# A gated-attention trunk: keys and four gates of the second layer by seven block products for eight, their results kept in device memory, the rotary swap on ScalarE

## The chip, the core and the metric

The kernel runs on one core of a Trainium2 chip. The metric is device time in microseconds (us): the median of several runs of the whole program. The profile comes from one further execution of the same program. The engines are called PE (TensorE, matmuls; PEld is its weight load), DVE (VectorE), ACT (ScalarE), POOL (GpSimd) and SP (SyncE, which issues all DMAs here).

## The reference

The input is a sequence of 1024 positions with 1024 features, in float32. Layer one is gated linear attention; layer two is dilated sliding-window attention over keys and values that are shared by its heads. Cut to what matters here, layer two computes:

```python
kv = x @ w_kv                              # 6 key tiles of 128 features, 6 value tiles
k, v = split(kv)
k = rope(k, pos)                           # x1*cos - x2*sin, x2*cos + x1*sin over halves of 64
q, g = split(x @ w_in)                     # 8 heads x 3 groups of queries, 8 gate tiles
q = rope(q, pos) * HEAD_DIM ** -0.5
for window, dilation in ((128, 1), (512, 4), (2048, 16)):
    o_g, lse_g = dilated_window_attention(q[group], k[group], v[group], window, dilation)
o = sum(softmax(lse) * o_g)                # three groups joined
y = (o * silu(g)) @ w_out
x = layer_norm(alpha * x + y)
```

Two key heads serve eight query heads: heads 0 to 3 use key head 0, heads 4 to 7 use key head 1.

## The kernel before, in words

**Arithmetic.** A product of float32 matrices is made of three matmuls in the type fp32r: each operand is split into a high part (`split_hi`, L612, an ACT copy) and a low part (`split_lo`, L615, a subtraction on DVE or POOL), and high x high, high x low and low x high are summed in PSUM (`mm3`, L642). The attention itself uses plain float32 matmuls.

**Tiles.** Features lie on the 128 partitions and positions along the free dimension, in halves of 512. `project` (L655) makes one 128-feature tile of a projection: it loads 512 KB of weights, splits them (`load_w_now`, L629), and for each half runs 8 x 3 matmuls of 128x512 into one PSUM bank; a function `evac` then takes the bank out. `project_tok` (L664) and `proj_v` (L1218) make values with positions on the partitions. SBUF is handed out in pages of 128x1024 (`page`, L618, 16 of them in the pool `p0` and 16 in `p1`) and in halves of that (`small`, L1053).

**Order.** The program is not issued in the order in which it is written. The class `Sched` (L141) records every operation; `order` (L254) then lays them out by a list schedule with a cost for each operation (`cost`, L543), a rule that a POOL operation and a DVE operation with two SBUF operands don't run at once (`shares_port`, L532), a limit on buffers, and priorities: the program's order, moved forward by `WEIGHTS` for weight loads and by `EVAC` for taking banks out. Operations recorded on `S.vp` go to DVE or POOL, those on `S.va` to DVE or ACT. All instructions are issued from line 452, so the profile shows that line for nearly all of them, and groups must be told apart by tile names. Buffers of one tag are handed out in the program's order.

**Stages.** Layer one (`layer_a`, L725) takes four heads in turn. `gate` (L883) makes the running sum of the log decays by a scan with a mask that restarts it every 128 positions. Then `out_ln` (L1067) makes the output projection and the layer norm, for one half of the positions at a time, and `emit_a` (L1547) writes the result x1 to SBUF, split, and to device memory (`x1d`). Layer two (`layer_b`, L1176) follows:

1. values of the first half of positions (`proj_v(0)`, `proj_v0`), L1265;
2. six key tiles by `project`, each taken out by `rope` (L1194), L1267; `rows` (L1257) between them turns x1 for the last stage;
3. values of the second half, L1271; values of key head 0 come back from device memory in the order of their groups (`load_v`, L1243); keys and values of key head 1 go out to device memory (`kvd`) until head 3 is done (`reload_kv`, L1281);
4. eight heads, L1515: `scores(u)`, for u < 4 the gate projection `g_proj(u)`, the next head's three query projections `q_proj(u+1)`, `attend(u)` and, for u < 4, `close(u)`, which multiplies by the gate; the gates of heads 4 to 7 come afterwards.

`rope` takes a PSUM bank out by three DVE products, one with the cosines (128x512) and two with the sines (64x512 each, reading the other half of the partitions), and one sum on DVE or POOL that also writes the result in the order of its group (`to_group`, L1165), so that the attention reads it contiguously.

Last come the output projection and layer norm of layer two.

Of the kernel before, what the change touches and what calls it, by code (L numbers as in the profile page):

```python
# [17 lines left out]
NK = 8  # L18
# [17 lines left out]
AHEAD = 0.35  # L36
RUNS, GATHER = 0.3, 1.0


# [558 lines left out]
def trunk(tc, xT, wP, wA, wA12, wAv3, w2, wO, wK, wV0, wV12, wB, wOB, par_d,  # L598
# [4 lines left out]
    wts = S.pool("wts")  # L603
    p0 = S.pool("p0")
    ps = S.pool("ps", space="PSUM")
    dram = S.pool("dram", space="DRAM")
# [118 lines left out]
    def layer_a(t2, t1, after):  # L725
        lmask = t2.tile([128, NLEV - 2, 32], U8, name="lmask")
        smask = t2.tile([128, 512], F32, name="smask")

# [424 lines left out]
    x1t = [dram.tile([128, D], F32, name=f"x1t{k}") for k in range(4)]  # L1153
    kvd = [dram.tile([128, T], F32, name=f"kvd{i}") for i in range(4)]

# [20 lines left out]
    def layer_b(xs, early):  # L1176
# [11 lines left out]
        S.vector.tensor_copy(below, tri[:, 1:2])  # L1188
        cosT = page(p0, F32, "cosT")
        S.sync.dma_start(cosT, cos_d)  # L1190
        sinT = page(p0, F32, "sinT")
        S.sync.dma_start(sinT, sin_d)
# [10 lines left out]
        K = [[page(p0, F32, f"K{c}{g}") for g in range(3)] for c in range(2)]  # L1203
        V = [[None] * 3 for _ in range(2)]

        def proj_v0(blocks):
            for c in range(2):
                if V[c][0] is None:
                    V[c][0] = page(p0, F32, f"V{c}0")

            def evac(j, acc):
                S.scalar.activation(blk(V[0][0], j), acc[:, 0:128], AF.Copy)
                S.vector.tensor_copy(blk(V[1][0], j), acc[:, 128:256])
            project_tok(wV0, xs, [(j, lambda x, j=j: blk(x, j)) for j in blocks], evac)

        def proj_v(half):  # L1218
# [12 lines left out]
            with S.later(-EVAC):  # L1231
                pgs = [page(p0, F32, "Vn") for _ in range(2)]
# [30 lines left out]


        proj_v(0)  # L1265
# [5 lines left out]
        proj_v(1)  # L1271
        for g in (1, 2):
            load_v(0, g)
        rows(6)
        rows(7)
        proj_v0(range(4, 8))
        for g in range(3):
            S.sync.dma_start(kvd[g], K[1][g])
        S.sync.dma_start(kvd[3], V[1][0])

        def reload_kv():  # L1281
            for g in range(3):
                K[1][g] = page(p0, F32, f"K1{g}")
                S.sync.dma_start(K[1][g], kvd[g])
            V[1][0] = page(p0, F32, "V10")
            S.sync.dma_start(V[1][0], kvd[3])
            load_v(1, 1)
            load_v(1, 2)


        BL = {0: [(n * 128, max(n - 1, 0) * 128, 128 if n == 0 else 256) for n in range(8)],
# [11 lines left out]
        def q_proj(u):  # L1303
            Q = [page(p0, F32, "Q") for _ in range(3)]
            U[u]["Q"] = Q
            for g in range(3):
                project(wB[u, g], xs, lambda half, acc: rope(Q[g], g, half, acc))


        def g_proj(u):  # L1310
            sg = page(p0, F32, "sg")
            U[u]["sg"] = sg

            def evac(half, acc):
                th = small("th", "t1", 2)
                S.scalar.activation(th, acc, AF.Tanh, scale=0.5)
                S.vector.scalar_tensor_tensor(sg[:, hs(half)], th, 1.0, acc, op0=OP.add, op1=OP.mult)
            project(wB[u, 3], xs, evac)

# [7 lines left out]
        def scores(u):  # L1327
            Q, Kc = U[u]["Q"], K[u // 4]
            P = {}
            sts = hp.tile([128, 2, 24], F32, name="sts", bufs=2)  # L1330
            for g in (2, 1, 0):
                step = 8 if g == 2 else 2
                for j0 in range(0, 8, step):
# [11 lines left out]
                    for j in range(j0, j0 + step):  # L1345
# [6 lines left out]
                        if g < 2:  # L1352
                            S.tensor.matmul(sc[:, o:o + nk], Q[g][:, qc:qc + 128], Kc[g][:, kc:kc + nk],
                                             start=True, stop=True)
# [60 lines left out]
        def attend(u):  # L1415
            P, cw, Vc = U[u]["P"], U[u]["cw"], V[u // 4]
            og = page(p0, F32, "og")
            U[u]["og"] = og
# [109 lines left out]
        for u in (4, 5, 6, 7):  # L1528
            if u == 7:
# [14 lines left out]
    layer_a(t2, t1, reload_og)  # L1544
    x1s = []

    def emit_a(et, r, t):  # L1547
# [6 lines left out]
        split_lo(lo[:, r], t, hi[:, r])  # L1554
        S.sync.dma_start(x1d[et][:, r], t)

    for half in range(2):
# [43 lines left out]
def _arrays(inputs):  # L1601
# [46 lines left out]
    a["cos"] = c(np.concatenate([cs, cs]))  # L1648
    a["sin"] = c(np.concatenate([sn, -sn]))
    q, k = np.meshgrid(r(128), r(256), indexing="ij")  # L1650
# [35 lines left out]
```

## Time and profile before

| what | value |
|---|---|
| median of 3 runs | 1154.25 us (1153.87 to 1154.63) |
| span of the profiled execution | 1152.7 us |
| mean granted PE clock | 0.998 of full speed |
| DMA traffic | 108.39 MB, mean 94 GB/s |

How to read the profile: the busy table gives each engine's busy time, its share of the span and its instructions. The chain follows the work that ended last back to what released each step. The groups give, for instructions of one kind, operation and tile, their count, busy time and mean in ns, then the idle time of the engine before them and what ended it. A matmul's duration is its latency; the next one starts before it ends.

### The profile page before, as it was taken

To read this page: it belongs to the slowest core of one execution; us is meant where nothing else is said; L and a number is where in the kernel's file an instruction comes from. 1 tells how busy PE (TensorE), PEld (TensorE's weight loads), DVE (VectorE), ACT (ScalarE), POOL (GpSimd) and SP (SyncE) were. 2 spreads that over 40 slices of the span, in tenths; PEclk is the share of its full clock that TensorE was granted. 3 is DMA by queue.
4 is the path that set the end of the run, shared out by engine and by line. 5 is a ranking of instruction groups with operands and counts; after the bars stand their busy time and mean duration, and the time that the engine had idled before them with its cause. 6 is when DMAs were issued, how large, how long until landed. Compare 5 with 4: busy or idle time off the path is not lost.

```text
span 1152.7 us, 19731 instructions
## 1 busy us (share of the span) xinstructions
PE 1142.8 (99%) x7780; PEld 975.2 (85%) x7780; DVE 820.3 (71%) x1634; ACT 449.1 (39%) x929; POOL 188.0 (16%) x139
## 2 busy tenths in 40 slices
PE   9999999999999999999999999999999999999997
PEld 9888888889988888888988888888888888888876
DVE  6286862786966699764366868686777878767678
ACT  5355431646463335311214242424222443444342
POOL 1000100112011120211020303030211312212200
PEclk9999999999999999999999999999999999999999
DMA  7211222111144365443611111121141111134544
GB/s 256 71 38 38 74 79 87 38 61 51 57 171 140 137 214 158 166 143 103 208 47 34 51 38 57 38 50 45 38 165 39 38 21 38 39 96 126 193 136 182
DMA packets 93372, 108.39 MB, mean 94 GB/s; under 512 B 43648, under 2 KB 61952, under 8 KB 93280
## 3 DMA queue, kind: packets, MB, share of 16 engines
q1 hardware_dynamic: 93280, 107.13, 29.6%
q8 instruction: 61, 1.00, 0.4%
q14 instruction: 31, 0.25, 0.1%
HBM read 85.94 MB, written 21.17 MB: 93 GB/s over the span
## 4 chain that ended last, share of the span: by engine, by line
PE 93%; DVE 4%; DMA 2%; ACT 1%; issue 1%; POOL 0%; DVEq 0%; ACTq 0%
PE acc L452 63%; PE po L452 9%; PE lv L452 8%; PE vac L452 7%; PE ms L452 4%; PE pro L452 2%; DMA wf<-in_wOB 2%; DVE rt L452 1%; DVE wl L452 1%; DVE x1l L452 0%; ACT wh L452 0%; DVE P L452 0%; DVE lnA L452 0%; ACT woh L452 0%; DVE wol L452 0%
## 5 line engine op out<-in xcount | busy, mean ns | idle before, releaser
L452 PE MATMUL acc<-x1h,wh 128*128 128x512 f32 x608 | 252.3, 415 | 0.0
L452 PE MATMUL acc<-x1h,wl 128*128 128x512 f32 x608 | 237.6, 391 | 0.0
L452 PE MATMUL acc<-x1l,wh 128*128 128x512 f32 x608 | 237.1, 390 | 0.0
L452 ACT ACTIVATE wh<-wf 128x1024 fp32r<-128x1024 f32 (+2 forms) x104 | 108.1, 1040 | 281.0 <-PE acc L452 194.8
L452 POOL TENSOR_TENSOR wl<-wf,wh 128x1024 fp32r<-128x1024 f32 x39 | 93.5, 2397 | 553.1 <-ACT wh L452 414.8
L452 ACT ACTIVATE P<-P,sts 128x128 f32<-128x128 f32 (+2 forms) x192 | 81.5, 426 | 139.6 <-DVE sts L452 139.3
L452 PEld LDWEIGHTS acc<-x1h,wl 128*128 128x128 f32 x608 | 114.1, 188 | 24.5
L452 PEld LDWEIGHTS acc<-x1l,wh 128*128 128x128 f32 x608 | 114.5, 188 | 21.3
L452 PEld LDWEIGHTS acc<-x1h,wh 128*128 128x128 f32 x608 | 114.4, 188 | 21.1
L452 DVE TENSOR_TENSOR wl<-wf,wh 128x1024 fp32r<-128x1024 f32 (+2 forms) x66 | 83.4, 1265 | 58.2 <-ACT wh L452 48.0
L452 PE MATMUL acc<-xh,wh 128*128 128x512 f32 x256 | 101.8, 397 | 0.0
L452 PE MATMUL acc<-xh,wl 128*128 128x512 f32 x256 | 99.8, 390 | 0.0
L452 PE MATMUL acc<-xl,wh 128*128 128x512 f32 x256 | 99.7, 390 | 0.0
L452 DVE TENSOR_TENSOR t<-acc,cosT 128x512 f32<-128x512 f32 x60 | 41.4, 689 | 65.7 <-PE acc L452 65.7
L452 DVE TENSOR_TENSOR t<-acc,sinT 64x512 f32<-64x512 f32 x120 | 82.5, 688 | 1.6
L452 PE MATMUL lv<-K,Q 128*64 128x64 f32 (+2 forms) x512 | 70.2, 286 | 0.0
L452 DVE CUSTOM_DVE_ANT_0 P<-lv,bmask 128x256 f32<-128x256 f32 (+1 forms) x128 | 46.7, 379 | 25.1 <-PE lv L452 23.7
L452 PEld LDWEIGHTS lv<-K,Q 128*128 128x128 f32 (+1 forms) x512 | 53.8, 163 | 10.0 <-issue 1.6
L452 PE MATMUL acc<-ogh,wh 128*128 128x512 f32 x152 | 60.1, 395 | 0.0
L452 PE MATMUL acc<-ogh,wl 128*128 128x512 f32 x152 | 59.2, 389 | 0.0
L452 PE MATMUL acc<-ogl,wh 128*128 128x512 f32 x152 | 59.2, 389 | 0.0
L452 PEld LDWEIGHTS acc<-xh,wl 128*128 128x128 f32 x256 | 48.0, 188 | 10.2
(252 smaller groups left out, 2233.4 us busy)
## 6 DMA issues: line engine op xcount, KB each, us to landing
wf<-in_wB SPq DMA_DIRECT2D x32, 512.0 KB
wf<-in_wA SPq DMA_DIRECT2D x24, 512.0 KB
wf<-in_wO SPq DMA_DIRECT2D x16, 512.0 KB
wf<-in_wOB SPq DMA_DIRECT2D x16, 512.0 KB
wf<-in_wV SPq DMA_DIRECT2D x12, 512.0 KB
res<-in_xT SPq DMA_DIRECT2D x16, 256.0 KB
x1d<-rt SPq DMA_DIRECT2D x16, 256.0 KB
out<-rt SPq DMA_DIRECT2D x16, 256.0 KB
```

Source lines behind the costliest of these rows:

```text
L452: getattr(handle[o.eng], meth)(*[conv(a) for a in args], **{k: conv(v) for k, v in kw.items()})
```

## The change

It has five parts.

1. **Seven products for eight.** The six key tiles and the gate tiles of heads 0 to 3 are made in five pairs by a scheme of Strassen's kind. A pair's weights are seen as blocks of (upper or lower four tiles of the model dimension) x (first or second feature tile), x1 as blocks of (upper or lower four tiles) x (first or second half of positions). `seven` makes seven block products of 4 x 3 matmuls each, on sums of blocks, instead of eight; four block results come out of sums of products.
2. **Sums of x1.** `sums` forms the four sums T1 to T4 of x1's blocks from the rows of the layer norm and from x1d read back, and keeps them split, in 16 pages of `p0`.
3. **Device memory.** All keys, the first group's values and the four gates go to device memory (`kd`, `vd0`, `sgd`) and come back before the heads that use them (`reload_kv(0)`, `reload_kv(1)`, `load_gate`). All four value projections come first, then the sums, then pairs of keys and gates in turn, with `rows` between.
4. **Rotary swap.** In `rope` the two sine products become two ACT copies that swap the halves of the partitions and one product on DVE or POOL. Group 1's queries are no longer reordered when written; the scores load them with a step of four elements.
5. **Room.** The cosine and sine pages, the pages `og` and the staging of keys lie in a new pool of four pages; the cosines load from 200 us on; the scan's mask is half as long, so each scan becomes two; a scratch area is made smaller.

The diff, cut to its core:

```diff
+    def spare(dt, name):
+        return px.tile([128, T], dt, name=name, tag="pg", bufs=4)
...
-                S.vector.tensor_tensor_scan(b[:, r], smask, mn, 0.0, op0=OP.mult, op1=OP.add)
+                for c0 in (0, 256):
+                    S.vector.tensor_tensor_scan(b[:, half * 512 + c0:half * 512 + c0 + 256], smask,
+                                                 mn[:, c0:c0 + 256], 0.0, op0=OP.mult, op1=OP.add)
...
-        def rope(pg, g, half, acc):
+        def rope(pg, g, half, acc, walked=(0, 1, 2)):
             r = hs(half)
             t1 = small("t1", "t1", 2)
             S.vector.tensor_mul(t1, acc, cosT[:, r])
             t2 = small("t2", "t2", 2)
-            S.vector.tensor_mul(t2[0:64, :], acc[64:128, :], sinT[64:128, r])
-            S.vector.tensor_mul(t2[64:128, :], acc[0:64, :], sinT[0:64, r])
-            S.vp.tensor_add(to_group(pg, g, half), tok_view(t1, g), tok_view(t2, g))
+            S.scalar.copy(t2[0:64, :], acc[64:128, :])
+            S.scalar.copy(t2[64:128, :], acc[0:64, :])
+            S.vp.tensor_mul(t2, t2, sinT[:, r])
+            if g in walked:
+                S.vp.tensor_add(to_group(pg, g, half), tok_view(t1, g), tok_view(t2, g))
+            else:
+                S.vp.tensor_add(pg[:, r], t1, t2)
...
+        def load_pair(src):
+            with S.later(-WEIGHTS):
+                a, b = (wts.tile([128, 1024], F32, name="wf", bufs=2) for _ in range(2))
...
+                a11, a12 = split(a)
+                hi, lo = (small("w22", "a", 13, FR) for _ in range(2))
+                split_hi(hi, b[:, R])
+                split_lo(lo, b[:, R], hi)
+                a22 = four(hi), four(lo)
+                S.vp.tensor_add(b[:, R], b[:, L], b[:, R])
+                S.vp.tensor_sub(b[:, L], a[:, L], b[:, L])
+                s3, s1 = split(b)
+                S.vp.tensor_sub(a[:, L], b[:, R], a[:, L])
+                S.vp.tensor_sub(a[:, R], a[:, R], a[:, L])
+                s2, s4 = split(a)
+            return dict(P1=a11, P2=a12, P4=a22, P7=s3, P5=s1, P6=s2, P3=s4)
...
+        def seven(src, evac):
+            w = load_pair(src)
...
+            acc = prod("P1", "a")
+            u = small("u1", "a", 13)
+            with late():
+                S.scalar.copy(u, acc)
+            acc = prod("P7", "b")
+            f = small("u2", "a", 13)
+            with late():
+                S.scalar.copy(f, acc)
+            acc = prod("P2", "a")
+            with late():
+                evac(0, 0, acc)
+            prod("P4", "b")
+            acc = prod("P5", "c")
+            with late():
+                S.vector.tensor_add(f, f, acc)
+            acc = prod("P6", "d")
+            with late():
+                S.vector.tensor_add(u, u, acc)
+                c21 = small("c", "a", 13)
+                S.vector.tensor_add(c21, u, banks["b"])
+                evac(1, 0, c21)
+                S.vp.tensor_add(f, u, f)
+                evac(1, 1, f)
+            acc = prod("P3", "c")
+            with late():
+                S.vector.tensor_add(u, u, acc)
+                evac(0, 1, u)
...
         proj_v(0)
         proj_v0(range(4))
+        proj_v(1)
+        proj_v0(range(4, 8))
+        sums()
...
         for g in range(3):
-            for c in range(2):
-                project(wK[2 * g + c], xs, lambda hf, acc, p=K[c][g]: rope(p, g, hf, acc))
-                rows(2 * g + c)
...
+            keys(g)
+            for et in range(3 * g, min(3 * g + 3, 8)):
+                rows(et)
+            if 2 * g < NG:
+                gates(2 * g)
...
+        reload_kv(0)
...
-            if u < 4:
-                g_proj(u)
...
-                if u < 4:
+                if u < NG:
+                    load_gate(u)
                     close(u)
             if u == 3:
-                reload_kv()
-        for u in (4, 5, 6, 7):
+                reload_kv(1)
+        for u in range(NG, 8):
...
+    def sums():
+        for k in range(4):
+            t, low = raws[k], raws[k + 4]
+            old, old2 = (small("old", "d", 4) for _ in range(2))
+            S.sync.dma_start(old, x1d[k][:, 0:512])
+            S.sync.dma_start(old2, x1d[k + 4][:, 0:512])
+            S.vp.tensor_sub(old, t, old)
+            keep("T1", k, old)
+            S.vp.tensor_sub(t, low, t)
+            keep("T3", k, t)
+            S.vp.tensor_sub(low, low, old)
+            keep("T2", k, low)
+            S.vp.tensor_sub(old2, old2, low)
+            keep("T4", k, old2)
```

`keep` splits a sum into its page. NG is 4; a further switch for queries by the same scheme, NQ, is 0, so the queries stay as they were.

More of the change, by code (lines that the diff above doesn't have):

```diff
@@ L37 @@
 RUNS, GATHER = 0.3, 1.0
+NG, NQ = 4, 0
 class Buf:
@@ L1188, in layer_b @@
         S.vector.tensor_copy(below, tri[:, 1:2])
[L1189 to L1192, printed above, removed]
-        def rope(pg, g, half, acc):
+        cosT, sinT = spare(F32, "cosT"), spare(F32, "sinT")
+        with S.hold(200.0):
+            S.sync.dma_start(cosT, cos_d)
+            S.sync.dma_start(sinT, sin_d)
+        def rope(pg, g, half, acc, walked=(0, 1, 2)):
             r = hs(half)
@@ new lines, in pure, with prod, late @@
+        def pure(k0, h):
+            return [(xs[k0 + k][0][:, hs(h)], xs[k0 + k][1][:, hs(h)]) for k in range(4)]
+        MOVING = dict(P1=lambda: pure(0, 0), P2=lambda: pure(4, 0), P3=lambda: pure(4, 1),
+                      **{p: lambda n=n: [quarter(n, k) for k in range(4)]
+                         for p, n in (("P4", "T4"), ("P5", "T1"), ("P6", "T2"), ("P7", "T3"))})
+        def seven(src, evac):
+            w = load_pair(src)
+            banks = {}
+            def prod(p, bank):
+                first = bank not in banks
+                if first:
+                    tag = {"a": "acc", "b": "lv", "c": "po", "d": "acc"}[bank]
+                    banks[bank] = ps.tile([128, 512], F32, name="sev", tag=tag, bufs=2)
+                acc = banks[bank]
+                hi, lo = w[p]
+                for k, (xh, xl) in enumerate(MOVING[p]()):
+                    with S.group():
+                        S.tensor.matmul(acc, hi[:, k, :], xh, start=first and k == 0, stop=False, skip_group_check=True)
+                        S.tensor.matmul(acc, hi[:, k, :], xl, start=False, stop=False, skip_group_check=True)
+                        S.tensor.matmul(acc, lo[:, k, :], xh, start=False, stop=(k == 3), skip_group_check=True)
+                return acc
+            def late():
+                return S.later(-EVAC)
+            acc = prod("P1", "a")
[25 more added lines that the diff above has]
+                evac(0, 1, u)
@@ L1262, in rows, with sigmoid_gate, keys @@
                 S.sync.dma_start(x1t[i][:, et * 128:et * 128 + 128], blk(t, i))
+        def sigmoid_gate(sg, acc):
+            th = small("th", "t1", 2)
+            S.scalar.activation(th, acc, AF.Tanh, scale=0.5)
+            S.vector.scalar_tensor_tensor(sg, th, 1.0, acc, op0=OP.add, op1=OP.mult)
+        def keys(g):
+            for c in range(2):
+                K[c][g] = spare(F32, f"K{c}{g}")
+            seven([wK[2 * g], wK[2 * g + 1]], lambda c, hf, acc: rope(K[c][g], g, hf, acc))
+            for c in range(2):
+                S.sync.dma_start(kd[c][g], K[c][g])
@@ L1312, in g_proj, with load_gate @@
             U[u]["sg"] = sg
[L1314 to L1318, printed above, removed]
+            project(wB[u, 3], xs, lambda half, acc: sigmoid_gate(sg[:, hs(half)], acc))
+        def load_gate(u):
+            sg = page(p0, F32, "sg")
+            U[u]["sg"] = sg
+            S.sync.dma_start(sg, sgd[u])
         def pieces(P, g, j0):
```

97 lines of the change are left out of this document (66 added, 31 removed).

## The prediction

> **What bounds the kernel now.** I read the page's busy table and chain first, then the chain in order of time, then the busy time by stage, then the groups by form.
>
> ```profile
> PE 1142.8 (99%) x7780; PEld 975.2 (85%) x7780; DVE 820.3 (71%) x1634; ACT 449.1 (39%) x929; POOL 188.0 (16%) x139
> ...
> PE 93%; DVE 4%; DMA 2%; ACT 1%; issue 1%; POOL 0%; DVEq 0%; ACTq 0%
> ...
> q1 hardware_dynamic: 93280, 107.13, 29.6%
> ```
>
> TensorE (PE) is busy for 99% of the span and carries 93% of the chain that ended last; the DMA engines are three tenths full. A busy PE may still be half empty, since matmuls overlap, so the chain in order of time (start, length, what, count) has to say at what pace they are issued:
>
> ```profile
> 453.32 22.42 PE acc L452 x144
> 476.18 10.91 PE acc L452 x48
> ...
> 498.88 10.91 PE acc L452 x48
> ...
> 532.93 21.80 PE vac L452 x96
> ...
> 718.57 1.08 PE lv L452 x32
> ...
> 720.52 2.23 PE po L452 x20
> ...
> 779.49 1.08 PE lv L452 x32
> ...
> 889.09 1.50 PE lv L452 x34
> ...
> 939.20 1.50 PE lv L452 x34
> ```
>
> One projection of one 128-feature tile is 2 halves x 8 tiles of the model dimension x 3 partial products = 48 matmuls, and takes 10.91 us: one matmul of 512 columns every 0.227 us. It is a steady stream with nothing between, in the stage that the change rewrites. So a matmul taken away there is worth its pace, provided that the other engines keep up. How near they are shows in the busy time by stage (window, length, then busy time and count of PE, PEld, DVE, ACT, POOL):
>
> ```profile
> 429.00:453.00 24.00, 23.56 (x103) 18.87 (x102) 22.26 (x33) 12.60 (x21) 0.44 (x1) 1.00 0.47 158
> 453.00:464.00 11.00, 11.00 (x93) 10.96 (x93) 10.36 (x21) 7.63 (x14) 0.00 (x0) 1.00 0.88 274
> 464.00:498.00 34.00, 34.00 (x158) 28.30 (x158) 23.51 (x31) 7.81 (x12) 8.38 (x4) 1.00 0.48 154
> 498.00:532.00 34.00, 34.00 (x157) 28.16 (x157) 22.18 (x24) 4.63 (x6) 7.20 (x3) 1.00 0.34 108
> ...
> 889.00:939.00 50.00, 50.00 (x299) 43.09 (x298) 41.14 (x117) 18.31 (x63) 13.14 (x10) 1.00 0.14 33
> ```
>
> VectorE (DVE) is full up to 464 (the tail of the first layer norm), two thirds full in the key stage, four fifths in the attention heads. The granted clock is 1.00 throughout. DVE is the only engine that could take PE's place.
>
> **The matmuls removed.** Six key tiles and four gate tiles are 10 projections, 480 matmuls, 109.1 us by the row of 10.91. Afterwards they are five pairs; a pair is 7 products x 4 tiles x 3 partial products = 84 matmuls for 96. 420 x 0.2273 = 95.5 us. Gain: 60 x 0.2273 = **13.6 us**. The mean of one in the groups is no price for this:
>
> ```profile
> L452 PE MATMUL acc<-x1h,wh 128*128 128x512 f32 x608 | 252.3, 415 | 0.0
> L452 DVE TENSOR_TENSOR wl<-wf,wh 128x1024 fp32r<-128x1024 f32 x61 | 80.4, 1319 | 58.2 <-ACT wh L452 48.0 <-PE ms L452 9.7
> L452 POOL TENSOR_TENSOR wl<-wf,wh 128x1024 fp32r<-128x1024 f32 x39 | 93.5, 2397 | 553.1 <-ACT wh L452 414.8 <-PE ms L452 117.6 <-PE lv L452 12.1
> L452 DVE TENSOR_TENSOR t<-acc,cosT 128x512 f32<-128x512 f32 x60 | 41.4, 689 | 65.7 <-PE acc L452 65.7
> L452 DVE TENSOR_TENSOR t<-acc,sinT 64x512 f32<-64x512 f32 x120 | 82.5, 688 | 1.6
> L452 DVE TENSOR_TENSOR rt<-rt,R 128x512 f32<-128x512 f32 x24 | 16.0, 683 | 0.3 <-ACT R L452 0.3
> L452 DVE SCALAR_TENSOR_TENSOR sg<-th,acc 128x512 f32<-128x512 f32 x16 | 10.9, 683 | 5.1 <-ACT th L452 5.1
> L452 ACT ACTIVATE wh<-wf 128x1024 fp32r<-128x1024 f32 x100 | 105.7, 1058 | 280.9 <-PE acc L452 194.8 <-issue 44.1 <-PE vac L452 30.1
> L452 ACT ACTIVATE th<-acc 128x512 f32<-128x512 f32 x16 | 9.4, 588 | 20.6 <-PE acc L452 20.6
> ```
>
> and, from the view of the tile that the keys are written through (shortest, median, longest),
>
> ```profile
> L452 DVE TENSOR_TENSOR K<-t,t x12: 693/1412/2182, 473.3 to 534.7; 128x512 f32<-128x512 f32 x12
> ```
>
> 415 ns is one matmul's latency, of which the next hides almost half; 60 of those would be 24.9 us, which the pace above excludes.
>
> **What the pairs add on DVE.** These rows give the prices: 0.69 us for a sum or product of 512 columns, from PSUM or SBUF alike; 1.32 for a low part of 1024; and for the rotary sum, walked into the order of group 0, 1 and 2, I take the last row's three: 0.69, 1.41, 2.18. A pair splits three weight tiles and a half one (3 x 1.32 + 0.69 = 4.6), forms four block sums (2.7) and five sums of products (3.4). Keys add four cosine and four sine products (5.5) and four walked sums: 2.8, 5.6 or 8.7. That is 19.0, 21.8 and 24.9 us for the three key pairs. A gate pair adds four gating operations of 0.683 instead: 13.4. Together 92.5 us of DVE beside 95.5 us of PE: DVE just fits, if it did everything itself. It is really less, because operations overlap, and more where GpSimd (POOL) works, as the timeline shows:
>
> ```profile
> 429.49 0.39 PE L452 MATMUL vac<-wh,x1h 128*128 128x512 f32 x1
> ...
> 461.85 0.68 DVE L452 TENSOR_TENSOR rt<-rt,R 128x512 f32<-128x512 f32 x1
> 462.45 0.68 DVE L452 TENSOR_TENSOR x1l<-rt,x1h 128x512 fp32r<-128x512 f32 x1
> ...
> 470.54 0.55 DVE L452 TENSOR_SCALAR rt<-rt,par 128x512 f32<-128x512 f32 x1
> ...
> 476.69 2.40 POOL L452 TENSOR_TENSOR wl<-wf,wh 128x1024 fp32r<-128x1024 f32 x1 [3.58 <-ACT wh L452]
> ...
> 477.91 1.73 DVE L452 TENSOR_TENSOR K<-t,t 128x512 f32<-128x512 f32 x1
> ```
>
> Two DVE operations that last 0.68 start 0.60 apart, an eighth less than I counted, so about 82 us. And a walked sum that began while POOL held 2.40 us of work took 1.73 instead of 0.69. I take the first as the rule and the second for a rival. ScalarE's share, 3 x 1.06 + 0.63 of splits, two copies out of PSUM at 0.59 and, for keys, eight swap copies, is 9.7 us in a pair of 19.1: hidden. The copies that PE waits for inside a pair (a bank is copied between two products that accumulate in it) have one product, 12 x 0.227 = 2.7 us, as cover, against 0.59 and at most one split of 1.06 ahead in ScalarE's queue: nothing.
>
> **The sums of feature halves.** All four value projections now come first: 2 x 21.80 and 2 x 11.51 (the row of 22.42 less 10.91) = 66.6 us, from 429.5 to 496. Beside them DVE finishes the layer norm (to about 471, when the last row is scaled), splits six weight tiles for values (7.9), copies values out (3), prepares the first pair (up to 7) and makes the sixteen half sums and their low parts: 32 x 0.60 = 19.2. From 471 that is at most 37 us, so 508, if nothing of it fits in before 471; each weight tile that is split earlier pulls it forward. The first products that need a sum (P7) begin at 496 + 2.7 = 499, the others 5 to 11 us later. Between 0 and 9 us of PE waiting, then; the order is laid out by a planner that sees these dependences, and ready halves of P7 can start, so I take **1 us** and keep 9 for the range. The extra queue entries (x1 read back, keys, values and gates stored and reloaded: about 10 MB more on engines that are 29.6% full) sit on the sync queue ahead of weight loads; the keys are needed only after the first query projection, 3 x 10.91 us later: nothing.
>
> **Attention.** Heads 0 to 3 lose the gate projection that PE could put into gaps. Does PE stay full without it? The chain answers: the same scores of successive heads start 60.92 apart with a gate (718.57, 779.49) and 50.11 apart without (889.09, 939.20); the difference, 10.81, is one projection of 10.91. Heads without a gate run as dense. DVE gets lighter there: per half two sine products of 0.688 go and one of 0.69 comes (it may go to POOL), and group 1's sum is no longer walked (1.41 to 0.69): 6 x 0.69 + 2 x 0.72 = 5.6 of 41.14 us per head. ScalarE takes 12 x 0.59 = 7.1 more on 18.31 of 50. No gain on the path, no loss. The gate scan of the first layer, cut in two, is DVE work beside a full PE: nothing.
>
> Group 1's queries are now loaded into PE with a step of four elements. No row shows a stepped weight load; the nearest are
>
> ```profile
> L452 PEld LDWEIGHTS lv<-K,Q 128*128 128x128 f32 x256 | 45.7, 189 | 7.7
> L452 PE MATMUL po<-PT,V 128*128 128x128 f32 x432 | 54.0, 276 | 0.8 <-DVE PT L452 0.8
> ```
>
> Half of these 256 loads, 128, would be stepped. The second group's matmuls of group 1 write PSUM with that same step and run mixed with unstepped ones at 0.112 us each (2.23 for 20). From that I take 0; the other end is a load twice as long and fully exposed, 128 x 0.189 = 24.2 us. The Trainium skill (SBUF — State Buffer, note on cachelines under Door 1: The DMA port swizzle) speaks against the step: a line holds 16 bytes and full rate needs two hits in it, which four fp32 elements of step never give. By it the loads would slow down, and the time would be one of rival (b)'s; no run here shows it yet.
>
> **Sum.** -13.6 + 1 = -12.6 us on a span of 1152.7, so 1140.1; the median of the runs before lies 1.55 above that span, so **1141.6** as a median, 1.1% faster. 0.2%, 2.3 us, is about what a measurement of this kernel can tell from no change.
>
> **Rivals.** (a) The half sums come late and PE waits at the first pair: +4 to +9, 1145 to 1150. For it: DVE's 22.26 of 24 and 10.36 of 11 before 464. Against: POOL is idle there (0.44 and 0.00). (b) Stepped weight loads cost. At a quarter of the end above, 6 us, the time is 1147.6; from 12.6 / 128 = 98 ns exposed per load the gain is gone; at 24.2 it is 1165. Against: PEld's loads lie beside matmuls. (c) The other side: in the key stage DVE and POOL get in each other's way and DVE becomes the bound. Each collision costs 1.73 - 0.69 = 1.04 us. The gain is gone when DVE needs 95.5 + 12.6 = 108.1 us, so with 15 collisions on top of the 92.5; with 25 the stage takes 118.5 us and the kernel 1141.6 + 23 = 1164.6. For it: some 56 more operations with two SBUF operands in the five pairs. Against: the overlapped pace leaves 13 us more. (d) That fewer matmuls don't mean less PE time is excluded by the pace; the count is fixed by the code.
>
> **Numbers.** Forecast, 1138 to 1145: 0.70. (a) 0.13. (b) 0.09, of it half faster, the rest split between the same and slower. (c) 0.08, nearly all slower. Faster by over 0.2% (below 1151.9): 0.70 + 0.13 + 0.04 = 0.87; same 0.04; slower 0.09. The range goes from 1138 (no wait at all, and a few of the small waits of attention gone with DVE's lighter load) to 1151, the end of (a) and the middle of (b); it leaves out about 0.13 above.
>
> **What would show it.** Right: the new products stream at 0.227, five pairs take 95 to 97 us from the last value projection to the first query projection, heads start 50 apart from the first on, DVE in the key stage is 80 to 90% busy. Wrong: PE gaps of microseconds with DVE as releaser before P7 (a) or spread over the key pairs (c), many DVE sums of 1.5 us or more there, or score loads of group 1 longer than 0.19 and heads over 51 us apart (b).

## The result and the profile after

| kernel | median, us | range | ratio to before (95% interval) |
|---|---|---|---|
| before | 1154.06 | 1153.64 to 1154.63 | 1 |
| after | 1161.16 | 1159.76 to 1162.24 | 1.0063 (1.0049 to 1.0077) |

The change makes the kernel 0.6% slower; the forecast was 1141.6, with 1138 to 1151 as its range. The profiled execution after spans 1160.1 us against 1152.7. The page after, its busy table, the chain by engine and the first DMA queue:

```profile
PE 1142.9 (99%) x7720; PEld 974.1 (84%) x7720; DVE 820.2 (71%) x1656; ACT 542.5 (47%) x1080; POOL 196.4 (17%) x157
...
PE 84%; DVE 9%; DMA 2%; ACT 2%; issue 2%; SPq 0%; DVEq 0%; ACTq 0%
...
q1 hardware_dynamic: 97600, 117.62, 32.5%
```

There are 60 instructions fewer on PE, and PE is busy for as long as before: something made it slower or kept it waiting inside its busy time. Its share of the chain falls from 93% to 84%, DVE's rises from 4% to 9%. The chain in order of time (start, length, what, count):

```profile
502.75 19.16 PE sev L453 x84
...
641.30 1.75 PE lv L453 x34
684.62 1.75 PE lv L453 x34
735.97 1.75 PE lv L453 x34
788.87 1.75 PE lv L453 x34
841.76 1.75 PE lv L453 x34
```

The first pair takes 19.16 us for 84 matmuls, 0.228 each: the seven products run at the forecast pace. The scores of the heads start 51.35, 52.90 and 52.89 apart, where 50 was forecast, and the first rows of a head's scores take 1.75 where they took 1.50. The loss is in the heads, and VectorE's load in the key stage is not the reason, as the busy time by stage shows (window, length, PE, PEld, DVE, ACT, POOL, granted clock, DMA share, GB/s):

```profile
450.00:500.00 50.00, 48.81 (x296) 43.68 (x295) 47.67 (x75) 29.53 (x51) 9.28 (x5) 1.00 0.70 220
500.00:550.00 50.00, 49.70 (x237) 40.95 (x236) 37.87 (x50) 26.97 (x39) 11.61 (x8) 1.00 0.43 143
550.00:600.00 50.00, 49.70 (x223) 40.44 (x222) 34.54 (x41) 22.17 (x31) 13.89 (x10) 1.00 0.52 169
```

DVE is full only from 450 to 500, where the half sums are made. In the stage of the pairs it is busy for 72.4 of 100 us, and PE waits for 0.3 in 50. The groups, shapes apart (busy, mean ns, idle before), and the view of the tile of queries (shortest, median, longest) show the two things that changed in the heads. The second line is that of the kernel before, the others are of the kernel after:

```profile
L453 PEld LDWEIGHTS lv<-K,Q 128*128 128x128 f32 x256 | 56.4, 254 | 6.3 <-DVE sts L453 0.8
...
L452 PE MATMUL ms<-ident,P 128*128 128x128 f32 x160 | 21.7, 272 | 0.0
...
L453 PE MATMUL ms<-ident,P 128*128 128x128 f32 x160 | 22.5, 273 | 4.9 <-DVE P L453 4.9
```

```profile
L453 PEld LDWEIGHTS lv<-K,Q x512: 132/162/333, 641.2 to 1026.7; 128*128 128x128 f32 x86, 128*64 128x64 f32 x85
```

The loads of query tiles take 254 ns in the mean where they took 189, and the longest takes 333. And the transposes of the probabilities (`ms<-ident,P`) waited 4.9 us for DVE, and 0.0 before. What DVE does ahead of one such gap, in the timeline, reads:

```profile
770.17 0.68 DVE L453 TENSOR_TENSOR t<-acc,cosT 128x512 f32<-128x512 f32 x1
770.97 1.19 ACT L453 ACTIVATE t<-acc 64x512 f32<-64x512 f32 x2
...
772.20 1.77 DVE L453 TENSOR_TENSOR t<-t,sinT 128x512 f32<-128x512 f32 x1 [1.34 <-ACT t L453]
...
775.57 0.69 DVE L453 TENSOR_TENSOR t<-acc,cosT 128x512 f32<-128x512 f32 x1 [0.88 <-PE acc L453]
777.58 0.69 DVE L453 TENSOR_TENSOR t<-t,sinT 128x512 f32<-128x512 f32 x1 [1.32 <-ACT t L453]
...
779.25 0.18 DVE L453 TENSOR_TENSOR mnB<-nat 128x8 f32<-128x8 f32 x1
...
781.49 0.69 DVE L453 TENSOR_TENSOR P<-P,cw 128x512 f32<-128x512 f32 x1
...
782.33 0.63 PE L453 MATMUL ms<-ident,P 128*128 128x128 f32 x4 [1.36 <-DVE P L453]
```

Between a cosine and a sine product DVE stands for 1.3 us and waits for ScalarE's two swap copies; behind those waits, in its order, stands the joining of the groups (from `mnB`, which begins the weights of the three groups, to `P<-P,cw`, which applies them), for which PE waits. The copies themselves start 0.12 us after the cosine product has ended, though both only read the bank `acc`.

The starts of the matmuls in the timeline cut the span into four stages. The second row is worked out: the kernel before with its four gate tiles (43.6 us) moved out of the heads and 13.6 us of matmuls removed.

| us | layer one, to the first value | values, keys, gates, first queries | first to last head's scores | from there to the last matmul |
|---|---|---|---|---|
| before | 429.5 | 175.6 | 384.1 | 156.0 |
| forecast without any wait | 429.5 | 205.6 | 340.5 | 156.0 |
| after | 432.6 | 208.6 | 356.4 | 155.1 |
| e1_walk | 432.4 | 208.6 | 349.8 | 152.9 |
| e2_noswap | 432.9 | 213.9 | 348.9 | 161.0 |
| e6_swap_keys | 431.6 | 208.6 | 344.9 | 159.5 |
| e10_told | 431.9 | 208.6 | 343.9 | 152.9 |
| e12_both | 429.7 | 208.7 | 343.6 | 152.8 |
| e14_eight_told | 432.1 | 219.0 | 343.2 | 152.0 |

After lost 3.1 us in layer one, 3.0 in the key stage and 15.9 in the heads, 21 us net of a slightly shorter end.

### The profile page after: what moved, and what is told of

Same layout as the page of the kernel before. It is cut to its first block, busy times and chain, and to the rows that moved or that the text cites. A ratio compares the mean times of both kernels' runs of the same rounds, so it can differ in the third digit from the quotient of the medians.

```text
span 1160.1 us, 19928 instructions
## 1 busy us (share of the span) xinstructions
PE 1142.9 (99%) x7720; PEld 974.1 (84%) x7720; DVE 820.2 (71%) x1656; ACT 542.5 (47%) x1080; POOL 196.4 (17%) x157
## 4 chain that ended last, share of the span: by engine, by line
PE 84%; DVE 9%; DMA 2%; ACT 2%; issue 2%; SPq 0%; DVEq 0%; ACTq 0%
PE acc L453 48%; PE lv L453 10%; PE po L453 9%; PE sev L453 7%; PE vac L453 5%; PE ms L453 4%; PE pro L453 3%; DVE rt L453 2%; DVE wl L453 2%; DMA wf<-in_wOB 1%; DVE wf L453 1%; ACT wh L453 1%; DVE x1l L453 1%; DMA nat<-std 1%; DMA wf<-in_wB 1%
## 5 line engine op out<-in xcount | busy, mean ns | idle before, releaser
L453 PE MATMUL acc<-x1h,wh 128*128 128x512 f32 x448 | 190.3, 425 | 0.0
L453 PE MATMUL acc<-x1h,wl 128*128 128x512 f32 x448 | 175.5, 392 | 0.0
L453 PE MATMUL acc<-x1l,wh 128*128 128x512 f32 x448 | 174.9, 390 | 0.0
L453 DVE TENSOR_TENSOR wl<-wf,wh 128x1024 fp32r<-128x1024 f32 (+2 forms) x84 | 107.3, 1279 | 52.1 <-ACT wh L453 42.0
L453 POOL TENSOR_TENSOR wl<-wf,wh 128x1024 fp32r<-128x1024 f32 x26 | 62.4, 2399 | 347.6 <-ACT wh L453 186.1
L453 PEld LDWEIGHTS acc<-x1h,wl 128*128 128x128 f32 x448 | 84.1, 188 | 18.3
L453 PEld LDWEIGHTS acc<-x1h,wh 128*128 128x128 f32 x448 | 85.1, 190 | 14.2
L453 PEld LDWEIGHTS acc<-x1l,wh 128*128 128x128 f32 x448 | 84.4, 188 | 14.7
L453 ACT ACTIVATE t<-acc 64x512 f32<-64x512 f32 x96 | 56.9, 593 | 61.7 <-DVE t L453 42.4
L453 PEld LDWEIGHTS lv<-K,Q 128*128 128x128 f32 (+1 forms) x512 | 64.5, 196 | 9.0 <-DVE P L453 1.4
```

What stands on the lines that cost most here:

```text
L453: getattr(handle[o.eng], meth)(*[conv(a) for a in args], **{k: conv(v) for k, v in kw.items()})
```

## The experiments

Each was timed in rounds beside the kernel before (1153.5 to 1154.4 in these rounds).

### The step and the swap, each undone

**e1_walk** writes group 1's queries in their order again and loads them without a step:

```diff
-                    project(wB[u, g], xs, lambda half, acc: rope(Q[g], g, half, acc, (0, 2)))
+                    project(wB[u, g], xs, lambda half, acc: rope(Q[g], g, half, acc))
...
-                            qb = Q[1][:, qc // 256, qc % 256:qc % 256 + 128] if g else blk(Q[0], j)
-                            S.tensor.matmul(sc[:, o:o + nk], qb, Kc[g][:, kc:kc + nk],
+                            S.tensor.matmul(sc[:, o:o + nk], Q[g][:, qc:qc + 128], Kc[g][:, kc:kc + nk],
```

> The change with one part undone: group 1's queries are again written in the order of their group, so the scores load them without a step. Theory S (stepped weight loads): in the changed kernel the 256 score matmul records of 128x256 and 128x128 take 8.8 us more of PE's time than before, so their pace comes back and the time falls from 1161.2 to about 1152; the gaps of 1.0 to 1.5 us before the transposes of P stay. Theory K (knock-on): the gaps are late scores too, so they go as well and the time falls to about 1146. Rival W (the swap on ScalarE is the whole loss): no change, 1161.

Measured: 1154.03 us, ratio 1.0003 (0.9994 to 1.0012). The step cost 7.1 us. In the view of the query tile the longest load is short again, and the groups show that the waits of the transposes stayed:

```profile
L453 PEld LDWEIGHTS lv<-K,Q x512: 132/162/192, 641.0 to 1019.1; 128*128 128x128 f32 x86, 128*64 128x64 f32 x85
```

```profile
L453 PE MATMUL ms<-ident,P 128*128 128x128 f32 x160 | 22.7, 274 | 6.0 <-DVE P L453 6.0
```

So the gaps before the transposes are not a consequence of slow loads. They are five, and PE is idle in each for 0.91 to 1.37 us. (The expectations count the same gaps from start to start of the matmuls, which makes them 1.07 to 1.53 us.)

**e2_noswap** keeps the step and takes the swap back (the signs in the sine table go back with it):

```diff
-            S.scalar.copy(t2[0:64, :], acc[64:128, :])
-            S.scalar.copy(t2[64:128, :], acc[0:64, :])
-            S.vp.tensor_mul(t2, t2, sinT[:, r])
+            S.vector.tensor_mul(t2[0:64, :], acc[64:128, :], sinT[64:128, r])
+            S.vector.tensor_mul(t2[64:128, :], acc[0:64, :], sinT[0:64, r])
```

> The change with the rotary swap undone: two sine products on VectorE out of PSUM again, with the sine table as before; the stepped loads stay. Rival W (the swap lengthens the rotary chain and puts the merge of the three groups late): the gaps before the transposes of P, some 6 to 7 us in heads 0 to 6, go and the time falls from 1161.2 to about 1154. Theory K (gaps come from late stepped scores): the time stays at 1161, or rises to 1165 if VectorE needs the relief. Theory S predicts the same as K here.

Measured: 1167.49, ratio 1.0121 (1.0107 to 1.0135). **e3_walk_noswap** has both edits:

> Both undone: only the seven products, the half sums, the new order and the stores to device memory are left of the change. If the matmuls removed are worth 13.6 us and the losses of layer one (3.1 us) and of the value and key stages (3.0 us) stay: 1154.1 - 13.6 + 6.1 = 1146.6. If the heads still wait without their gate projections as cover: 1150 or more.

Measured: 1161.03, ratio 1.0059 (1.0046 to 1.0073). Without the swap the kernel is 6.3 and 7.0 us slower. The stage table shows both sides: the heads are 7.5 us shorter (e2 against after), and the transposes wait for nothing in the group of e2_noswap, so the swap does make the gaps:

```profile
L453 PE MATMUL ms<-ident,P 128*128 128x128 f32 x160 | 23.5, 273 | 0.0
```

But values, keys and first queries take 5.3 more and the end 5.9 more. In the first queries PE waits 2.97 us, up to 617.88, for a bank that DVE has yet to take out. The swap helps there and is paid for in the heads.

**e4_before_step** puts the step alone, with the queries not reordered, into the kernel before:

> The kernel before with one part of the change alone: group 1's queries stay in the order of positions and the scores load them with a step of four elements. Theory S: 128 stepped loads cost PE 8.8 us, 1154.1 + 8.8 = 1163; a load record of 0.33 us instead of 0.19. If the lighter VectorE sums (0.7 us each on 16) give something back: 1161. If the step costs nothing by itself: 1154.

Measured: 1162.69, ratio 1.0078 (1.0065 to 1.0090), 9.0 us slower than the kernel before. The step is a loss by itself, whatever else the change does.

### The other parts alone

**e5_before_scans** puts the split scan alone into the kernel before:

```diff
-                S.vector.tensor_tensor_scan(b[:, r], smask, mn, 0.0, op0=OP.mult, op1=OP.add)
+                for c0 in (0, 256):
+                    S.vector.tensor_tensor_scan(b[:, half * 512 + c0:half * 512 + c0 + 256], smask,
+                                                 mn[:, c0:c0 + 256], 0.0, op0=OP.mult, op1=OP.add)
```

> The kernel before with only the split scan of the first layer (16 scans of 256 for 8 of 512, the mask half as long). In all kernels with the seven products so far the first layer takes 2.4 to 3.1 us longer than before. If the split scan is the cause: 1153.7 + 3 = 1156.7, with the first value projection at about 432 instead of 429.5. If it comes from another part (buffers moved, the cosines loaded at 200 us): 1153.7.

Measured: 1156.02, ratio 1.0021 (1.0012 to 1.0030). The groups of before, then of this kernel:

```profile
L452 DVE TENSOR_TENSOR_SCAN b<-smask,mn 128x512 f32<-128x512 f32 x8 | 9.8, 1225 | 0.3
```

```profile
L452 DVE TENSOR_TENSOR_SCAN b<-smask,mn 128x256 f32<-128x256 f32 x16 | 11.3, 716 | 0.3
```

Half a scan takes 716 ns, not 612. That is 1.5 us more of DVE in layer one, yet the first value projection starts 3.1 us later, at 432.6, as it does after (the profiled execution was 1.6 us above the median of this kernel). The loss is spread: no idle time of PE there that the kernel before lacks is over 0.46 us.

**e6_swap_keys** is e1_walk with the swap for keys and the first head's queries only; the other queries use two sine products again:

```diff
+            if not swap:
+                S.vector.tensor_mul(t2[0:64, :], acc[64:128, :], sinT[64:128, r])
+                S.vector.tensor_mul(t2[64:128, :], acc[0:64, :], sinT[0:64, r])
+                S.vp.tensor_sub(to_group(pg, g, half), tok_view(t1, g), tok_view(t2, g))
+                return
```

> Group 1 walked again as in the first of the variants (1154.0), and the swap on ScalarE only for keys and the first head's queries; the other queries take the two sine products on VectorE. In the profile without any swap the gaps before the transposes of P (five of 1.1 to 1.5 us) are gone from the heads, while VectorE falls behind in the key stage. If the swap in the heads causes the gaps: 1154.0 - 6 = 1148. If VectorE's higher load in the heads and at the end costs as much: 1154 or more.

Measured: 1155.73, ratio 1.0020 (1.0011 to 1.0029). The heads are as dense as hoped, 344.9 us against 349.8, but the end takes 6.6 us more. The busy time by stage there:

```profile
1040.00:1050.00 10.00, 7.22 (x40) 5.96 (x38) 7.13 (x15) 4.39 (x9) 2.56 (x2) 0.94 0.63 206
1050.00:1060.00 10.00, 8.77 (x44) 6.85 (x44) 8.50 (x23) 4.08 (x9) 1.09 (x2) 0.88 0.21 45
```

PE is idle there for 0.92 and 1.86 us before and after the transposes of the last head, and the granted clock falls to 0.94 and 0.88 of full speed in the mean: it is one stretch of 3.41 us at 0.50, from 1048.90 on. In e1_walk PE is busy for the whole of these two windows at a clock of 1.00. Giving DVE its work back moved the waiting, it did not remove it.

**e7_gates_in_heads** is e1_walk with the gates of heads 0 to 3 by eight products inside the heads again; only keys go by seven.

```diff
-            if 2 * g < NG:
-                gates(2 * g)
...
+            if u < 4:
+                g_proj(u)
...
-                    load_gate(u)
```

> Group 1 walked again, and the gates of heads 0 to 3 projected inside the heads as before, by eight products; only the keys go by seven. 24 matmuls more on PE: +5.4 us of work. If the heads wait because they lost the gate projection as cover, their gaps (heads 0 to 3: about 5 us) go and the key stage gets shorter: about 1154, the same as with the gate pairs. If the cover was not needed: 1154.0 + 5.4 = 1159.4.

Measured: 1154.55, ratio 1.0005 (0.9997 to 1.0014), the same as e1_walk although it does 24 matmuls (5.4 us) more. Its gaps of over 1 us in the heads are two, both in heads without a gate; heads with one start 61.0 apart, as before. A gate projection inside the head covers the late joining; taking it out saves matmuls and opens the gaps.

**e8_eight** is e1_walk with keys and gates by eight ordinary products and without the half sums; order, stores, swap and scans stay.

```diff
+            for n in range(2):
+                project(src[n], xs, lambda hf, acc, n=n: evac(n, hf, acc))
...
-        sums()
```

> Group 1 walked again, and everything else of the change kept (order, stores to device memory, swap on ScalarE) but for the seven products: keys and gates go by the ordinary eight, and the half sums are left out. This prices the scheme itself: 60 matmuls more, 13.6 us, less what the pairs cost elsewhere. If the scheme nets its full 13.6: 1167.6. If VectorE's work for the pairs costs the 3.7 us that the value and key stages lost: 1164. If the scheme nets nothing: 1154.

Measured: 1165.16, ratio 1.0099 (1.0087 to 1.0112). Seven products for eight are worth 11.1 us here (1165.16 against the 1154.03 of e1_walk).

### The cause of the gaps

The timeline after suggested a cause that undoing the swap can't tell from plain work: the planner. It prices two reads of one bank as independent, so it lets copies and cosine product run at once and puts the sine product right behind; in the trace the copies wait for the cosine product. The waits view after says how often (us in total, times, longest):

```profile
ACT t L453 <- DVE t L453: 43.9, 27, 4.2
...
DVE t L453 <- ACT t L453: 28.0, 32, 2.1
```

The Trainium skill (PSUM — Partial Sum Buffer, "PSUM bank collisions raise a hardware error") says that two engines must not touch one bank and quadrant at once, two readers among them, and that the compiler's scheduler adds a dependency for it. The trace agrees: in none of the 48 pairs of a cosine product and its copies do the two overlap, and where a copy waited for DVE, it started 0.03 to 0.12 us after the product's end, with DVE named as releaser. A releaser is found from semaphores, so it is the program that holds the two apart; no run here shows them reading at once.

**e10_told** is e1_walk with that order told to the planner. The instructions stay the same:

```diff
             S.vector.tensor_mul(t1, acc, cosT[:, r])
+            cos = len(S.ops) - 1
             t2 = small("t2", "t2", 2)
             S.scalar.copy(t2[0:64, :], acc[64:128, :])
+            S.ops[-1].behind = (cos,)
             S.scalar.copy(t2[64:128, :], acc[0:64, :])
+            S.ops[-1].behind = (cos,)
...
+            deps |= set(getattr(o, "behind", ()))
             o.deps = deps
```

> The walked version with one thing changed: the planner is told that the two swap copies on ScalarE start only when the cosine product on VectorE has read the same PSUM bank, which is what the trace shows (copies start 0.09 us after its end). The instructions are the same, only their order can move. Theory: the planner priced the copies as simultaneous, so VectorE stands before the sine product for 1.3 us and the joining of the groups comes late; with the right price it puts other work there, the gaps of 1.07 to 1.53 us before the transposes shrink below 0.5, heads start 50.2 to 50.8 us apart instead of 51.7, and the time falls by 2 to 5 us, to 1149 to 1152. Rival: the joining is late because of its DMAs and ScalarE's share of the work, the gaps stay and the time stays within 1 us of 1154.

Measured: 1146.54, ratio 0.9936 (0.9925 to 0.9948): 7.5 us less, more than expected. The timeline and the group of the transposes:

```profile
765.20 0.69 DVE L454 TENSOR_TENSOR t<-acc,cosT 128x512 f32<-128x512 f32 x1 [1.82 <-PE acc L454]
766.07 1.23 DVE L454 TENSOR_TENSOR wl<-wf,wh 128x1024 fp32r<-128x1024 f32 x1 [0.18 <-ACT wh L454]
767.29 0.69 DVE L454 TENSOR_TENSOR t<-t,sinT 128x512 f32<-128x512 f32 x1
...
768.93 0.18 DVE L454 TENSOR_TENSOR mnB<-nat 128x8 f32<-128x8 f32 x1
...
771.18 0.69 DVE L454 TENSOR_TENSOR P<-P,cw 128x512 f32<-128x512 f32 x1
```

```profile
L454 PE MATMUL ms<-ident,P 128*128 128x128 f32 x160 | 22.1, 273 | 0.1
```

A weight tile is now split while ScalarE copies, the joining of the same head is done 10 us earlier than after (771.18 against 781.49, the head itself starting 2.8 us earlier), and the transposes wait for next to nothing. The scores of heads 1 to 3 start 50.1 apart. The waits of DVE themselves are fewer but not gone: between 640 and 1000 us DVE waits for the copies 18 times, 15.8 us in total, where e1_walk has 26 and 24.6. What went is that the joining stood behind them.

**e11_swap_first** issues the copies first and the cosine product after them, and tells the planner so.

```diff
-            S.vector.tensor_mul(t1, acc, cosT[:, r])
             t2 = small("t2", "t2", 2)
             S.scalar.copy(t2[0:64, :], acc[64:128, :])
             S.scalar.copy(t2[64:128, :], acc[0:64, :])
+            swap = len(S.ops) - 1
+            S.vector.tensor_mul(t1, acc, cosT[:, r])
+            S.ops[-1].behind = (swap,)
```

> The walked version with the two swap copies issued ahead of the cosine product, the planner told of that order. If two engines that read one bank are kept apart, the cosine product starts about 0.1 us after the second copy ends, as the copies did after it before; VectorE then makes cosine, sine and sum in one go, without the wait of 1.3 us between them, and the gaps before the transposes shrink: 1147 to 1151. If readers are not kept apart, the cosine product starts while the copies run. Rival as for the kernel told of the order: the gaps stay, within 1 us of 1154.

Measured: 1146.45, ratio 0.9935 (0.9923 to 0.9946), just below the range expected. The timeline shows that now the cosine product is the one that waits:

```profile
620.42 1.20 ACT L454 ACTIVATE t<-acc 64x512 f32<-64x512 f32 x2 [3.38 <-PE acc L454]
...
621.65 0.69 DVE L454 TENSOR_TENSOR t<-acc,cosT 128x512 f32<-128x512 f32 x1 [2.04 <-ACT t L454]
```

Whichever reader comes first, the other follows it. Which one does makes no difference to the time; that the plan knows it does.

### Whether the losses add

**e9_scan** is e1_walk with whole scans; the mask takes a page of the new pool that is idle in layer one.

```diff
-        smask = t2.tile([128, 256], F32, name="smask")
+        smask = spare(F32, "smask")[:, 0:512]
```

> The walked version (e1_walk) with one scan of 512 again in place of two of 256 in layer one; the mask takes a page of the new pool that is idle then. Theory: the split scan is what makes layer one end 2.5 to 3 us later, so the first value projection starts at 429.5 to 430 again instead of 432.4, and the time is 1151.0 to 1152.0 against 1154.0. Rival: the split explains little of it (earlier loading of the cosines, the moved pages), and the time stays within 1 us of 1154.

Measured: 1151.07, ratio 0.9974 (0.9965 to 0.9982), 3.0 us below e1_walk; the first value projection starts at 429.7. **e12_both** is e10_told with this edit:

> Walked queries, the planner told of the order of the two readers, and one scan of 512 in layer one: the three repairs together. If they lie in stages that do not touch, the gains add: 1146.5 less 3.0 to 3.3 is 1143.2 to 1143.5, 11 us below the kernel before. If the planner lays out later stages differently once layer one ends earlier, part is lost: 1144.5 to 1146.

Measured: 1144.56, ratio 0.9917 (0.9904 to 0.9931). That beats both kernels. It is 2.0 below e10_told, so the second case holds at its edge: of the 3.0 us that whole scans gave e9_scan, 1.0 is not kept. **e13_after_told** is the changed kernel, step and all, with the planner told:

> The changed kernel with its step in the query loads kept, and only the planner told of the order of the two readers. If the step's cost and the late joining of the groups add, the time is that of the walked and told kernel (1146.5) plus the 7.1 to 9.0 us that the step cost in the two pairs of kernels measured so far: 1153.5 to 1155.5, and the gaps of 1 to 1.5 us before the transposes are gone. If the slow loads hid part of the gaps, or made them, it is outside that: under 1152 or over 1157.

Measured: 1155.87, ratio 1.0013 (1.0004 to 1.0022): 5.3 below after, 9.3 above e10_told, and 0.4 above the range for losses that add. The gaps before the transposes are gone. What one loss costs depends on whether the other is there: the step costs 7.1 us with the untold plan and 9.3 with the told one, the untold plan 5.3 with the step and 7.5 without. So the two losses overlap by about 2 us. **e14_eight_told** is e8_eight with the planner told:

> Walked queries and the planner told, but keys and gates by eight ordinary products each, without the half sums (everything else of the change stays). If seven products for eight save their 60 matmuls in full, this kernel takes 1146.5 plus 13.6 less 1.4 (the gap of 1.37 us at the half sums, which go too), so 1158 to 1159. If the pairs cost more than that gap (evacuation, splits, stores that compete), the difference stays at the 11.1 us that the untold pair of kernels showed or below: 1157.6 or less.

Measured: 1155.73, ratio 1.0018 (1.0009 to 1.0026). With no gap in the heads on either side, the scheme's net worth is 9.2 us: the second case, and further below 13.6 than the 11.1 of the untold pair. The stage table places it, against e10_told: 10.4 us gained in the stage of values, keys and gates, 1.6 given back later in heads and end. Telling the planner was worth 9.4 us in this kernel (e8_eight against e14_eight_told).

## Why the prediction was wrong, step by step

**The matmuls removed: right.** 60 fewer, at 0.228 us each in the stream.

**VectorE beside the pairs, rival (c): right, with room.** It was busy for 72.4 of 100 us where 82 to 92.5 of 95.5 were counted and 80 to 90% was named as the sign, and PE did not wait for it among the pairs. Part of the surplus is a misread row: 693, 1412 and 2182 ns are the shortest, median and longest of twelve walked sums, not the prices of the three groups. In the trace before, group 0 takes 0.69 us and groups 1 and 2 take 1.10 while POOL is idle, and each of the six sums that run beside a weight split on POOL takes 1.03 to 1.09 more (1.73, and 2.13 to 2.18). With 1.10 for groups 1 and 2 the count is 5.5 us lower, 87.0. Collisions of rival (c)'s kind were thus in the row already; after, one of the twelve sums of keys shows one, with 1.82 us.

**The half sums, "1 us", rival (a): the size was nearly right, the mechanism in part.** DVE is full, as (a) had it, busy for 47.67 of 50 us. But PE does not wait for the first sums of P7: it is idle for 1.19 us up to 499.62 in the last value projection, until DVE has copied values out of a bank, and that copy stands behind four sums of the first pair's weights (3.93 us from 495.43 on). The whole stage is 3.0 us over its 205.6. Of the rest, two waits of 0.25 lie inside pairs, between the first product and the next one in its bank, for ScalarE's copy, which was put at nothing with one product as cover; there only four transposes lay between. What is left was not traced to a wait. The extra DMAs were taken at nothing and not tried by themselves; e14_eight_told has all of them but those of the half sums and is 1.4 us above the kernel before, less than the split scan alone costs.

**"I take 0" for the stepped loads: failed, the largest term.** The row it rested on was a matmul that writes PSUM with a step; nothing there says how weights are read from SBUF with one. Measured: 7.1 us (after against e1_walk), 9.0 (e4_before_step against before) and 9.3 (e13_after_told against e10_told), which is 55 to 73 ns for each of 128 loads, about half of the 0.13 us by which one became longer in the mean. Rival (b) had the mechanism, its place and nearly the price (6 us at a quarter of the end), but 9 in 100; the quarter had no row behind it, so that its price came near was luck. The need for two hits in a line, by which the note on cachelines of the Trainium skill (SBUF — State Buffer, under Door 1: The DMA port swizzle) spoke against the step, was borne out by loads of 308 to 333 ns against 189.

**"No gain on the path, no loss" in attention: failed, the second term.** The pace of heads without a gate, 50.11, was a fair measure of PE's work, and e10_told and e12_both reach 50.1. What failed was counting the swap as 7.1 us of ScalarE time and 5.6 us less of DVE time. It also puts a wait between two DVE products, and behind a waiting DVE stands the joining of the groups. That the copies run behind the cosine product and the planner does not know it costs 5.3 us with the step (after against e13_after_told) and 7.5 without (e1_walk against e10_told).

**The scan "beside a full PE: nothing": failed, a small term.** It cost 2.0 to 3.0 us (e12_both, e5_before_scans, e9_scan), spread over small losses and not in one wait.

Together: from 1161.16 the planner's blind wait takes 5.3, the step 9.3, the scan 2.0, taken away in this order, and 1144.56 is left, 3.0 above the forecast. By its stages, e12_both is 3.2 above the row without any wait, and nearly all of it is the stage of values and keys (208.7 against 205.6): layer one is 0.2 late, and heads and end together take 496.4 against 496.5. As the forecast held 1 us of wait, the account closes to about 1 us. Why the pairs give 1.6 us back in heads and end against e14_eight_told is not settled; it was not traced to a wait.

## What to carry to other kernels

A row prices an edit only if it shows the same access: a step on a matmul's output says nothing of a step on a weight load, and a rule that speaks against the edit then weighs more than that row. When work is moved from one engine to another that reads the same PSUM bank, ask when it can start and whether the plan knows, not only how long it takes; if an order is written by a planner, the trace's waits that the plan doesn't hold are the first thing to look for. And a wait that seems to belong to an engine's load may be one of order: undoing the work shifted the loss to another place, telling the plan took PE's wait away.

## What the runs showed of the hardware

- An fp32 weight load of 128x128 with a step of four elements takes 308 to 333 ns, without a step 189 in the mean (192 at most in e1_walk). Of the difference, 55 to 73 ns a load, about half, reach the matmul stream.
- ScalarE's copies and VectorE's product on one PSUM bank ran one after the other in either order, with 0.03 to 0.12 us between them where one waited for the other.
- The granted clock stood at half for 3.41 us after idle times of PE of 0.92 and 1.86 us with four transposes between them (e6_swap_keys, matmuls 0.43 us apart for 0.227), for 6.83 us with idle times of 0.89 and 1.86 (e3_walk_noswap), and for 3.41 us after a single one of 2.97 (e2_noswap, from 618.35). Single ones of up to 1.37 us in e1_walk left it at 1.00, and so did 1.86, 1.04 and 0.51 within 6 us in e2_noswap (1057.8 to 1063.8). So the lengths alone do not tell; what else decides was not tried.
- A walked sum of two SBUF operands on VectorE took 1.03 to 1.09 us longer beside a weight split on GpSimd (0.69 to 1.73, 1.10 to 2.13 and more; the key stage before).
- A scan of 256 columns took 716 ns, one of 512 took 1225: each half costs 0.1 us more than half of the whole, 1.7 us for the sixteen, and the kernel lost 2.0 to 3.0.
